# Diagonal blocks copied once each, token norms a projection earlier, and the order of rows and query norms in a DeltaNet layer

## The chip, the cores and the metric

The kernel runs on one core of a Trainium2 chip. The metric is the device time of one execution in microseconds (us). The kernel before takes 2926.78 us, the median of three runs (2923.34 to 2927.39).

The engines are named as the profile names them: PE (TensorE, matmuls; PEld is its weight load), DVE (VectorE), ACT (ScalarE), POOL (GpSimd) and SP (SyncE, which here only issues DMAs). Each engine works through its own queue in order, so an instruction that waits holds up all that stand behind it on that engine. L307 is line 307 of the kernel before; from L183 on, the changed kernel's lines have other numbers.

## The reference

One layer of a trunk on 2048 tokens of width 1024, all in float32: a gated DeltaNet mixer, then a squared-ReLU MLP, then a final norm. Cut to what matters here:

```python
h = rms_norm(x, norm_mix)
proj = h @ w_in                                       # q, k, v, z (8 heads of 128 each), b, a
q, k, v = split(silu(causal_conv4(proj[..., :3 * 1024])))
q, k = l2_normalize(q), l2_normalize(k)
# per head, in chunks:
lower = strict(k_beta @ k.T * decay)
u, w = solve(lower + I, [v * beta, k_beta * exp(gc)]) # unit lower triangular
v_new = u - w @ state
o = q_dec @ state + (q @ k.T * decay) @ v_new
state = state * g_last + k_dec.T @ v_new
x = x + (rms_norm(o) * norm_w * silu(z)) @ w_out
x = x + square(relu(rms_norm(x) @ w_up)) @ w_down
out = rms_norm(x)
```

The kernel uses chunks of 128 tokens, which gives the same numbers as the reference's 64.

## The kernel before

**Blocks, halves, pairs.** The tokens are worked in two blocks of 1024; each goes through `mixer` and then `mlp_block`. A mixer does two halves of 512 tokens (`s`), and in each half four pairs of heads (`h`). A pair has six projections of 512 columns, two heads each of k, q and v (`conv_part`), and each projection is 24 matmuls of 512 columns (L117 to L119, three partial products for each of eight slices). ACT copies the projection out of PSUM (L303, L304), DVE does three multiply-adds of the causal convolution (L307), ACT a tanh (L310) and DVE a product (L311).

**A pair's own work.** From k, `key_matrices` makes the 128x128 matrices `mt` of eight chunks (L429 on PE, L431 and L439 on DVE). `invert_diagonal` inverts the 32x32 diagonal blocks. Four ACT copies (L322) lay the blocks out in `xc`, each block repeated R = 4 times (1024 elements a partition); a DVE transpose (L325) turns them into `pr`; and 31 rows of a product and a sum each (L333, L335) follow on DVE. It is a generator, `rows_of`, that hands the rows out a few at a time. The rest of the inversion (`invert`: L345, L347, L365, L373, L376, L386, L392), transposes of k and v (L469, copied out by ACT at L472) and q times k (L478, L480) belong to `prepare2`. This is a generator too, `stages`, and runs while the next pair projects.

**The chain.** `wind_up` ends a pair while the next one winds up. It does two gate projections (`gate`) and the query norms: ACT squares q (L450), PE sums it (L452), and DVE reads the sum (L454), all through a PSUM bank of the tag `kq`. Then comes `chain`, a recurrence over four chunks of two heads: L496 on PE, `y` on DVE (L498), L505 on PE, `vr` on ACT (L507), L511 on PE, the state on DVE (L512). `fill` puts rows of the next pair between its steps. For the first pair of a block there is no pair to wind up, and its rows all stand at its end in the program.

**Token norms.** During the first half the tokens of the second are normed, 128 in each pair. A DMA fetches `xt` after the first projection; after the second, `norm_transpose` does squares (L180), a reciprocal root, `xn` (L181) and four transposes (L186, PSUM tag `po`), and after the fourth the other four.

**Weights.** In the first half of block 0 each projection's weights come from the input (`wr`, two buffers, L100), POOL splits them into a high and a low part (L90, L91), and SP saves the result (L104); later halves load the saved parts (L109).

**Order.** The program is a list that the framework sorts within each engine's queue by its own estimate, so the written order says only roughly what stands where. PSUM has eight banks: three for projections (`pj`), three for `kq`, two for `po`.

Of the kernel before, what the change touches and what calls it, by code (L numbers as in the profile page):

```python
# [7 lines left out]
F32 = mybir.dt.float32  # L8
# [8 lines left out]
P = 128  # L17
D = 1024
# [4 lines left out]
HB = 512  # L23
HT = HB // P
HP = 2
NC = HP * HT
# [7 lines left out]
def tile_kernel(ctx: ExitStack, tc: tile.TileContext, x, w_in, w_out, w_up, w_down, n_mlp, n_fin, consts, out):  # L34
# [142 lines left out]
    def norm_transpose(i, src, xn, wcol, hh, hl, tag):  # L177

        ssq = sm.tile([P, 1], F32, name="ssq", tag="ssq", bufs=3)
        act.activation(xn, src, AF.Square, accum_out=ssq)  # L180
        dve.tensor_scalar_mul(xn, src, rstd_of(ssq))  # L181
        ti = slice(i * P, (i + 1) * P)
        for k4 in range(0, KS, 4):  # L183
            ps = big(tag)
            for k in range(4):
                pe.transpose(ps[:, k * P:(k + 1) * P], xn[:, (k4 + k) * P:(k4 + k + 1) * P], ident)  # L186
            for k in range(4):
                src_, w = ps[:, k * P:(k + 1) * P], wcol[:, k4 + k:k4 + k + 1]
                act.activation(hh[:, k4 + k, ti], src_, AF.Copy, scale=w)
                dve.scalar_tensor_tensor(hl[:, k4 + k, ti], src_, w, hh[:, k4 + k, ti].bitcast(F32),  # L190
                                         op0=MULT, op1=SUB)
            yield
# [120 lines left out]
    def invert_diagonal(ap, u):  # L313

        R = 32 // NC
        mt = u["mt"]
        xc = wp.tile([P, 32, R, NC], F32, name="xc", tag="xt", bufs=4)
        for b in range(4):  # L320
            r = slice(32 * b, 32 * b + 32)
            act.copy(xc[r], mt[r, :, 32 * b:32 * b + 32].rearrange("p t i -> p i t").unsqueeze(2)  # L322
                     .to_broadcast([32, 32, R, NC]))
        pr = wp.tile([P, 32, 32], F32, name="pr", tag="xt", bufs=4)
        dve.transpose(pr.rearrange("p i j -> p (i j)"), xc.rearrange("p i r t -> p (i r t)"))  # L325
        pool.memset(pr.rearrange("p i j -> p (i j)")[:, 0:1024:33], 1.0)  # L326
        tt = ap.tile([P, NC, 32], F32, name="tt", tag="tt")
        pool.tensor_copy(tt.rearrange("p c j -> p (c j)"), e0)
        yield
        tmp = ap.tile([P, NC, 32], F32, name="tmp", tag="tmp", bufs=1)  # L330
        for i in range(1, 32):
            n = i // R + 1
            dve.tensor_tensor(tmp[:, 0:n, 0:i + 1], tt[:, 0:n, 0:i + 1],  # L333
                              pr[:, i, 0:i + 1].unsqueeze(1).to_broadcast([P, n, i + 1]), op=MULT)
            dve.tensor_reduce(tt[:, 0:n, i], tmp[:, 0:n, 0:i + 1], axis=mybir.AxisListType.X, op=ADD)  # L335
            if i % 2 or i > 16:
                yield
        u["tt"] = tt
# [244 lines left out]
    def mixer(blk, hT):  # L583
        with tc.tile_pool(name="ap", bufs=2) as ap:
# [11 lines left out]
            def wind_up(stages, rows_of, sb, h, hT, qkv, gt, u):  # L596

                def fill(n):
                    for _ in range(n):
                        next(rows_of, None)  # L600

                fill(1)
                z = [gate(ap, hT, h, sb)]
                for _ in stages:
                    pass
                z.append(gate(ap, hT, h + 1, sb))
                for j in range(HP):
                    query_norms(ap, u, qkv[0], j)
                os_ = chain(ap, h, u, fill)
                return [(sb, h + j, os_[j], z[j]) for j in range(HP)]  # L610

            def stages_of(sb, h, hT, qkv, gt, u):
                return prepare2(ap, sb, h, *qkv, gt, u, ub, t64)

            gt = None
            for s in range(2):
                sb = 2 * blk + s
                for h in range(0, NH, HP):
                    qkv, n = [], 0
                    stages = stages_of(*prev) if prev is not None else iter(())  # L620
                    next(stages, None)
                    if s == 0 and h == 0:
                        hT2 = half_tiles()
                    for part in (1, 0, 2):
                        d = ap.tile([P, HP * HB], F32, name=f"c{part}", tag=f"c{part}")
                        qkv.append(d)
                        for j in range(HP):
                            conv_part(ap, hT, part, h + j, d[:, j * HB:(j + 1) * HB], sb)
                            n += 1
                            next(stages, None)  # L630
                            if s == 0 and h == 0 and n <= 3:
                                if n == 1:
                                    gt = {}
                                    g_steps = gates(ap, sb, hT, gt)
                                next(g_steps)


                            if n == 3:
                                u = prepare(ap, sb, h, gt)
                                key_matrices(u, qkv[0], 0)  # L640
                            if n == 4:
                                key_matrices(u, qkv[0], 1)
                                key_norms(u)
                                rows_of = invert_diagonal(ap, u)
                                finish_ready()
                            if blk == 0 and s == 1 and n in (2, 5):
                                split_out(h // HP * 2 + n // 5)
                            if s == 0 and n == 1:
                                xt = wp.tile([P, D], F32, name="xt", tag="xt", bufs=4)
                                r0 = (sb + 1) * HB + h // HP * P  # L650
                                sp.dma_start(xt, x[r0:r0 + P, :])
                            if s == 0 and n == 2:
                                xt_steps = norm_transpose(
                                    h // HP, xt, wp.tile([P, D], F32, name="xn", tag="xt", bufs=4), nmix, *hT2, "po")
                            if s == 0 and n in (2, 4):
                                next(xt_steps)
                            if s == 0 and h == NH - HP and n >= 4:
                                if n == 4:
                                    gt2 = {}
                                    g_steps = gates(ap, sb + 1, hT2, gt2)  # L660
                                next(g_steps, None)
                    if prev is not None:
                        ready += wind_up(stages, rows_of, *prev)
                    for _ in rows_of:
                        pass
                    prev = sb, h, hT, (qkv[1], qkv[0], qkv[2]), gt, u
                if s == 0:
                    for _ in g_steps:
                        pass
                    hT, gt = hT2, gt2  # L670
# [224 lines left out]
```

## Time and profile before

| what | value |
|---|---|
| median of three runs | 2926.78 us |
| the profiled execution's own time | 2925.43 us |
| its span, first to last instruction | 2923.6 us |
| PE busy | 2772.0 us (95%) |
| DVE busy | 1551.5 us (53%) |
| ACT busy | 1024.6 us (35%) |
| POOL busy | 727.9 us (25%) |
| mean granted clock of PE | 0.971 of full speed |

The span is 1.8 us shorter than that execution's time. A share of the whole span says little here: the mixers (0 to about 820 us and about 1500 to 2230 us) and the MLPs have different limits, and PE's idle time lies nearly all in the mixers. So the profile is read stage by stage, by what PE waits for.

### The profile page before, as it was taken

The page shows a single profiled execution, that of the slowest core. Times are in us where ns is not written, and L with a number is a line of the kernel's source. Part 1 is how long each engine was busy: PE and PEld are TensorE (multiplying, and loading weights), DVE is VectorE, ACT ScalarE, POOL GpSimd, SP SyncE. Part 2 cuts the span into 40 slices and gives each one's busy share as a digit, 9 for nine tenths or more (in the row PEclk, how much of TensorE's full clock was granted, in tenths as well). Part 3 has the DMA queues.
Part 4 walks back from the last instruction along what each step waited for, and adds up shares of the span by engine and source line. Part 5 has one row for each costly group of instructions (what it writes and reads, how often), then busy time and mean ns, then how long its engine had stood idle before and what let it go on. Part 6 is the DMA issues. An engine that isn't in the chain of part 4 may idle for free.

```text
span 2923.6 us, 38571 instructions
## 1 busy us (share of the span) xinstructions
PE 2772.0 (95%) x14584; PEld 2294.2 (78%) x14584; DVE 1551.5 (53%) x3814; ACT 1024.6 (35%) x2274; POOL 727.9 (25%) x646
## 2 busy tenths in 40 slices
PE   7688989999999999999998999999999999999998
PEld 6577777777788888888877778788777888888887
DVE  7877677763434334333486776666533333343345
ACT  4455545553221211211246655555422112112112
POOL 6444222110142332332211111111004323323321
PEclk9889999999999999999999999999999999999999
DMA  6444455565521111111254434334572111111111
GB/s 235 174 159 173 159 174 180 180 201 198 185 72 37 58 51 37 58 51 38 64 200 141 145 114 151 139 135 146 173 260 87 44 44 58 45 43 58 46 42 65
DMA packets 77482, 337.52 MB, mean 115 GB/s; under 512 B 8560, under 2 KB 8816, under 8 KB 55792
## 3 DMA queue, kind: packets, MB, share of 16 engines
q1 hardware_dynamic: 58480, 292.98, 29.7%
q10 hardware_dynamic: 18816, 42.08, 4.2%
q8 instruction: 114, 1.87, 0.3%
q14 instruction: 72, 0.59, 0.1%
HBM read 271.98 MB, written 63.05 MB: 115 GB/s over the span
## 4 chain that ended last, share of the span: by engine, by line
PE 72%; DVE 15%; ACT 9%; issue 2%; DMA 1%; POOL 1%; ACTq 0%; POOLq 0%; DVEq 0%; SPq 0%
PE pj L118 12%; PE pj L117 12%; PE pj L119 12%; PE kq L119 8%; PE kq L118 8%; PE kq L117 8%; ACT xc L322 4%; DVE tmp L333 3%; DVE c L307 3%; DVE tt L335 2%; PE kq L511 1%; PE kq L505 1%; PE po L117 1%; PE po L119 1%; PE kq L429 1%
## 5 line engine op out<-in xcount | busy, mean ns | idle before, releaser
L117 PE MATMUL pj<-hh,w 128*128 128x512 f32 x2048 | 822.1, 401 | 0.0
L118 PE MATMUL pj<-hh,w 128*128 128x512 f32 x2048 | 818.9, 400 | 0.0
L119 PE MATMUL pj<-hl,w 128*128 128x512 f32 x2048 | 813.6, 397 | 0.0
L117 PEld LDWEIGHTS pj<-hh,w 128*128 128x128 f32 x2048 | 391.4, 191 | 77.4
L119 PEld LDWEIGHTS pj<-hl,w 128*128 128x128 f32 x2048 | 390.0, 190 | 79.0 <-issue 0.6
L118 PEld LDWEIGHTS pj<-hh,w 128*128 128x128 f32 x2048 | 392.0, 191 | 76.0 <-issue 0.4
L740 ACT ACTIVATE r<-pj 128x512 f32<-128x512 f32 x128 | 76.6, 599 | 1066.6 <-PE pj L119 1066.6
L743 DVE TENSOR_TENSOR ul<-r,uh 128x512 fp32r<-128x512 f32 x128 | 140.9, 1100 | 482.9 <-ACT uh L742 482.9
L119 PE MATMUL kq<-dl,uh 128*128 128x512 f32 x992 | 386.8, 390 | 0.0
L118 PE MATMUL kq<-dh,ul 128*128 128x512 f32 x992 | 386.7, 390 | 0.0
L117 PE MATMUL kq<-dh,uh 128*128 128x512 f32 x992 | 386.6, 390 | 0.0
L783 DVE TENSOR_TENSOR x<-kq,x 128x512 f32<-128x512 f32 x256 | 176.7, 691 | 211.4 <-PE kq L119 208.7
L307 DVE SCALAR_TENSOR_TENSOR c<-raw,cst,c 128x512 f32<-128x512 f32 x288 | 239.4, 835 | 78.3 <-ACT c L304 75.1
L91 POOL TENSOR_TENSOR w<-wr,w 128x1024 fp32r<-128x1024 f32 x106 | 260.8, 2460 | 7.1
L90 POOL TENSOR_SCALAR w<-wr 128x1024 fp32r<-128x1024 f32 x106 | 114.3, 1079 | 590.1 <-PE po L119 299.1
L783 DVE TENSOR_TENSOR x1h<-kq,x1h 128x512 f32<-128x512 f32 x256 | 176.6, 691 | 155.7 <-PE kq L119 155.4
L90 POOL TENSOR_SCALAR dh<-wr 128x1024 fp32r<-128x1024 f32 x62 | 64.2, 1051 | 655.6 <-PE kq L118 622.7
L117 PEld LDWEIGHTS kq<-dh,uh 128*128 128x128 f32 x992 | 186.2, 188 | 40.4 <-DVE rm L145 1.3
L118 PEld LDWEIGHTS kq<-dh,ul 128*128 128x128 f32 x992 | 186.2, 188 | 39.4
L119 PEld LDWEIGHTS kq<-dl,uh 128*128 128x128 f32 x992 | 186.2, 188 | 38.8
L333 DVE TENSOR_TENSOR tmp<-tt,pr 128x2 f32<-128x2 f32 (+30 forms) x496 | 164.5, 332 | 9.9 <-POOL pr L326 0.5
L91 POOL TENSOR_TENSOR dl<-wr,dh 128x1024 fp32r<-128x1024 f32 x62 | 147.3, 2394 | 0.5
(313 smaller groups left out, 3545.4 us busy)
## 6 DMA issues: line engine op xcount, KB each, us to landing
w<-wi SPq DMA_DIRECT2D x96, 1024.0 KB, 4.9
wi<-w SPq DMA_DIRECT2D x32, 1024.0 KB, 4.8
wr<-in_w_up SPq DMA_DIRECT2D x64, 512.0 KB, 3.6
w<-wo SPq DMA_DIRECT2D x32, 1024.0 KB, 5.9
wr<-in_w_down SPq DMA_DIRECT2D x64, 512.0 KB, 3.5
wr<-in_w_in SPq DMA_DIRECT2D x32, 512.0 KB, 5.8
qe<-eg_d ACTq DMA_DIRECT2D x16, 512.0 KB, 3.8
o_d<-z2s ACTq DMA_DIRECT2D x32, 256.0 KB, 2.7
```

Of the source, the lines that this page charges most:

```text
L90: pool.tensor_scalar(dst_h, src, 1.0, 0.0, op0=MULT, op1=ADD)
L91: pool.tensor_tensor(dst_l, src, dst_h.bitcast(F32), op=SUB)
L117: pe.matmul(ps, ah, bh, start=first and i == 0, stop=False)
L118: pe.matmul(ps, al, bh, start=False, stop=False)
L119: pe.matmul(ps, ah, bl, start=False, stop=last and i == n - 1)
L307: dve.scalar_tensor_tensor(dst, raw[:, k:k + HB], cw[:, 4 * f + k:4 * f + k + 1], dst, op0=MULT, op1=ADD)
L322: act.copy(xc[r], mt[r, :, 32 * b:32 * b + 32].rearrange("p t i -> p i t").unsqueeze(2) .to_broadcast([32, 32, R, NC]))
L333: dve.tensor_tensor(tmp[:, 0:n, 0:i + 1], tt[:, 0:n, 0:i + 1], pr[:, i, 0:i + 1].unsqueeze(1).to_broadcast([P, n, i + 1]), op=MULT)
L335: dve.tensor_reduce(tt[:, 0:n, i], tmp[:, 0:n, 0:i + 1], axis=mybir.AxisListType.X, op=ADD)
L740: act.activation(r, ps, AF.Relu)
L743: dve.tensor_tensor(ul[:, hs], r, uh[:, hs].bitcast(F32), op=SUB)
L783: dve.tensor_tensor(dst, ps, dst, op=ADD)
```

## The change

Five things change.

- **Diagonal blocks.** `xc` holds each block once (256 elements a partition), in a buffer of the tag `z`; the DVE transpose reads it four times over through a repeated axis. The `xt` buffers lose one user.
- **Token norms.** `norm_transpose` gives way once more after `xn`. The DMA of `xt` and the buffer for `xn` stand ahead of a pair's projections, squares and `xn` behind the first, the transposes behind the second and the fourth as before.
- **The first pair's rows.** They are no longer run at its end. In the second pair of a block's first half, 12 steps of them stand behind the first projection and the remainder behind the second; `stages` of the first pair starts behind the second projection.
- **Query norms.** They leave `wind_up` and stand behind the pair's own fifth and sixth projection.
- **Half tiles.** `half_tiles()` for the second half is called ahead of the loop.

```diff
@@ norm_transpose
         act.activation(xn, src, AF.Square, accum_out=ssq)
         dve.tensor_scalar_mul(xn, src, rstd_of(ssq))
+        yield
@@ invert_diagonal
-        xc = wp.tile([P, 32, R, NC], F32, name="xc", tag="xt", bufs=4)
+        xc = ap.tile([P, 32, NC], F32, name="xc", tag="z", bufs=1)
...
-            act.copy(xc[r], mt[r, :, 32 * b:32 * b + 32].rearrange("p t i -> p i t").unsqueeze(2)
-                     .to_broadcast([32, 32, R, NC]))
+            act.copy(xc[r], mt[r, :, 32 * b:32 * b + 32].rearrange("p t i -> p i t"))
...
-        dve.transpose(pr.rearrange("p i j -> p (i j)"), xc.rearrange("p i r t -> p (i r t)"))
+        dve.transpose(pr, xc.unsqueeze(2).to_broadcast([P, 32, R, NC]))
@@ wind_up
-                for j in range(HP):
-                    query_norms(ap, u, qkv[0], j)
@@ the loop over pairs
-                    next(stages, None)
+                    late = s == 0 and h == HP
+                    if not late:
+                        next(stages, None)
+                    if s == 0:
+                        xt = wp.tile([P, D], F32, name="xt", tag="xt", bufs=4)
+                        r0 = (sb + 1) * HB + h // HP * P
+                        sp.dma_start(xt, x[r0:r0 + P, :])
+                        xt_steps = norm_transpose(
...
-                            next(stages, None)
+                            if s == 0 and n in (1, 2, 4):
+                                next(xt_steps)
+                            if late and n < 3:
+                                for _ in range(12 * n):
+                                    next(rows_of, None)
+                            if not late or n > 1:
+                                next(stages, None)
...
+                            if n > 4:
+                                query_norms(ap, u, qkv[1], n - 5)
...
-                    for _ in rows_of:
-                        pass
+                    if prev is not None:
+                        for _ in rows_of:
+                            pass
```

What stands in the queues shows it at three places. On PE, in the sixth pair of block 0 (the chain of the states S_88 and S_90), the query sums `kq<-ones,sq` stood in front of the chain's first matmuls. Before:

```order
L118 MATMUL pj<-hh,w_5175 128x512
L119 MATMUL pj<-hl,w_5175 128x512
L452 MATMUL kq<-ones,sq 128x1 x4
L502 MATMUL po<-S_88,qe 128x128
L502 MATMUL po<-S_90,qe 128x128
L117 MATMUL pj<-hh,w_5442 128x512
L118 MATMUL pj<-hh,w_5442 128x512
L119 MATMUL pj<-hl,w_5442 128x512
L117 MATMUL pj<-hh,w_5442 128x512
L452 MATMUL kq<-ones,sq 128x1 x4
L496 MATMUL kq<-S_88,c_3975 128x128
L496 MATMUL kq<-S_90,c_3975 128x128
```

Now they stand two gate projections earlier, and the chain begins:

```order
L118 MATMUL pj<-hh,w_5207 128x512
L119 MATMUL pj<-hl,w_5207 128x512
L496 MATMUL kq<-S_88,c_3991 128x128
L496 MATMUL kq<-S_90,c_3991 128x128
L502 MATMUL po<-S_88,qe 128x128
L502 MATMUL po<-S_90,qe 128x128
L505 MATMUL kq<-y,ub 128x128 x2
L117 MATMUL pj<-hh,w_5458 128x512
```

The matmuls of the next projection that stood between the sums and L505 are behind L505 now; in both orders DVE has about 18 of the next pair's rows in front of `y`.

On DVE, `xn` of the second pair's tokens (block 0) stood among the first pair's rows, beside the second pair's first convolution (c_774). Before:

```order
L139 SCALAR_TENSOR_TENSOR rst<-rt,rst 128x1
L335 TENSOR_REDUCE tt<-tmp 128x4
L135 TENSOR_SCALAR rt<-rst,rh 128x1
L333 TENSOR_TENSOR tmp<-tt,pr 128x4x15
L139 SCALAR_TENSOR_TENSOR rst<-rt,rst 128x1
L335 TENSOR_REDUCE tt<-tmp 128x4
L181 TENSOR_SCALAR xn<-xt,rst 128x1024
L333 TENSOR_TENSOR tmp<-tt,pr 128x4x16
L307 SCALAR_TENSOR_TENSOR c_774<-raw,cst,c_774 128x512
```

Now both first `xn` stand beside the very first convolution (c_264):

```order
L181 TENSOR_SCALAR xn<-xt,rst 128x1024
L139 SCALAR_TENSOR_TENSOR rst<-rt,rst 128x1
L135 TENSOR_SCALAR rt<-rst,rh 128x1
L139 SCALAR_TENSOR_TENSOR rst<-rt,rst 128x1
L135 TENSOR_SCALAR rt<-rst,rh 128x1
L139 SCALAR_TENSOR_TENSOR rst<-rt,rst 128x1
L308 SCALAR_TENSOR_TENSOR c_264<-raw,cst,c_264 128x512
L181 TENSOR_SCALAR xn<-xt,rst 128x1024
L308 SCALAR_TENSOR_TENSOR c_264<-raw,cst,c_264 128x512 x2
L312 SCALAR_TENSOR_TENSOR c_264<-raw,c_264 128x512
```

On SP, in the first half of block 0, loads of raw weights (`wr`) and saves of split ones (`wi`) alternated. Before:

```order
L100 DMA wr<-in_w_in 128x1024
L104 DMA wi_0_120<-w_611 128x2048
L100 DMA wr<-in_w_in 128x1024
L104 DMA wi_1_121<-w_652 128x2048
L100 DMA wr<-in_w_in 128x1024
L104 DMA wi_2_114<-w_779 128x2048
```

Up to about the sixteenth projection they go in twos now:

```order
L100 DMA wr<-in_w_in 128x1024 x2
L104 DMA wi_0_120<-w_611 128x2048
L104 DMA wi_1_121<-w_660 128x2048
L100 DMA wr<-in_w_in 128x1024 x2
L104 DMA wi_2_114<-w_713 128x2048
L104 DMA wi_3_115<-w_821 128x2048
```

A save waits for its split on POOL, so the first load of two is queued behind one split more than it was.

## Rows read from the trace of the kernel before

**Rows 1.** Windows by stage: busy us of PE, PEld, DVE, ACT, POOL; granted clock, DMA, GB/s.

```profile
0.00:158.00 158.00, 115.81 (x616) 94.07 (x616) 120.08 (x273) 72.30 (x136) 81.89 (x92) 0.90 0.59 209
158.00:335.00 177.00, 153.66 (x957) 126.29 (x956) 139.65 (x429) 89.54 (x219) 64.51 (x62) 0.92 0.44 153
335.00:639.00 304.00, 280.12 (x1827) 234.50 (x1826) 215.69 (x620) 163.75 (x387) 64.89 (x84) 0.96 0.54 186
639.00:1505.00 866.00, 857.40 (x3968) 707.95 (x3968) 348.10 (x638) 199.94 (x427) 227.33 (x138) 0.99 0.26 84
1505.00:1613.00 108.00, 94.52 (x548) 77.55 (x547) 76.46 (x246) 61.72 (x119) 15.04 (x37) 0.95 0.49 172
1613.00:2061.00 448.00, 424.98 (x2781) 355.19 (x2779) 315.71 (x1048) 253.29 (x606) 49.00 (x99) 0.97 0.40 140
```

**Rows 2.** PE's waits in the whole span: us in total, times, longest us.

```profile
PE po L186 <- DVE xn L181: 25.9, 2, 15.9
PE kq L496 <- DVE n L454: 19.8, 8, 5.5
PE po L469 <- ACT vt L472: 13.0, 10, 5.0
PE kq L452 <- ACT sq L450: 11.7, 6, 3.2
PE po L186 <- ACT o L530: 11.5, 3, 8.1
PE kq L172 <- DVE xn L167: 8.5, 1, 8.5
...
PE kq L505 <- DVE y L498: 5.5, 10, 0.9
```

**Rows 3.** PE's timeline: start us, us; idle before and its releaser in brackets.

```profile
96.94 0.47 PE L186 MATMUL po<-cst,xn 128*128 128x128 f32 x1 [15.94 <-DVE xn L181]
...
564.49 0.58 PE L496 MATMUL kq<-S,c 128*128 128x128 f32 x1 [3.93 <-DVE n L454]
```

**Rows 4.** ACT's copies by line and shape: count, busy us, mean ns, idle before.

```profile
L322 ACT COPY xc<-mt 32x1024 f32<-32x1024 f32 x64 | 129.9, 2029 | 31.6 <-DVE mt L439 24.0 <-DMA o_d<-z2s 6.7
...
L347 ACT COPY tcm<-tr 128x256 f32<-128x256 f32 x16 | 10.8, 675 | 9.8 <-DVE tr L345 4.7 <-DVE rq L139 3.1 <-DVE nq L524 1.9
```

**Rows 5.** DVE's block transposes by line and shape, columns as in rows 4.

```profile
L325 DVE STREAM_TRANSPOSE pr<-xc 128x1024 f32<-128x1024 f32 x16 | 19.9, 1246 | 38.1 <-ACT xc L322 38.1
...
L345 DVE STREAM_TRANSPOSE tr<-tt 128x256 f32<-128x256 f32 x16 | 7.1, 441 | 0.3
```

**Rows 6.** Windows of DVE alone, up to each block's first chain: busy us, then clock.

```profile
29.00:158.00 129.00, 99.07 (x240) 0.87 0.57 199
...
1506.00:1613.00 107.00, 75.57 (x243) 0.95 0.48 170
```

**Rows 7.** DVE's timeline in the sixth pair of block 0, from pr to y.

```profile
551.33 1.25 DVE L325 STREAM_TRANSPOSE pr<-xc 128x1024 f32<-128x1024 f32 x1 [2.07 <-ACT xc L322]
...
558.61 2.21 DVE L333 TENSOR_TENSOR tmp<-tt,pr 128x33 f32<-128x33 f32 x1
...
564.28 0.15 DVE L454 TENSOR_SCALAR n<-kq 128x4 f32<-128x4 f32 x1
...
565.91 0.60 DVE L498 SCALAR_TENSOR_TENSOR y<-kq,neg,vt 128x128 f32<-128x128 f32 x2
```

**Rows 8.** DVE's convolution step in 0 to 639 us, then in 1505 to 2061 us.

```profile
L307 DVE SCALAR_TENSOR_TENSOR c<-raw,cst,c 128x512 f32<-128x512 f32 x144 | 132.3, 922 | 35.7 <-ACT c L304 34.2
...
L307 DVE SCALAR_TENSOR_TENSOR c<-raw,cst,c 128x512 f32<-128x512 f32 x144 | 107.1, 747 | 42.6 <-ACT c L304 40.9
```

**Rows 9.** POOL's split in 0 to 639 us; raw weight loads: count, KB, us to landing.

```profile
L91 POOL TENSOR_TENSOR w<-wr,w 128x1024 fp32r<-128x1024 f32 x40 | 97.9, 2448 | 1.6
L90 POOL TENSOR_SCALAR w<-wr 128x1024 fp32r<-128x1024 f32 x40 | 44.9, 1122 | 75.5 <-PE pj L119 69.7 <-DMA dt__498<-gc_d 2.5 <-DMA wr<-in_w_in 2.0
...
wr<-in_w_in SPq DMA_DIRECT2D x32, 512.0 KB, 5.8
```

More of the change, by code (lines that the diff above doesn't have):

```diff
@@ L613, in stages_of @@
                 return prepare2(ap, sb, h, *qkv, gt, u, ub, t64)
-            gt = None
+            gt, hT2 = None, half_tiles()
             for s in range(2):
@@ L620, in mixer @@
                     stages = stages_of(*prev) if prev is not None else iter(())
-                    next(stages, None)
-                    if s == 0 and h == 0:
-                        hT2 = half_tiles()
+                    late = s == 0 and h == HP
[6 more added lines that the diff above has]
+                        xt_steps = norm_transpose(
+                            h // HP, xt, wp.tile([P, D], F32, name="xn", tag="xt", bufs=4), nmix, *hT2, "po")
                     for part in (1, 0, 2):
@@ L647, in mixer @@
                                 split_out(h // HP * 2 + n // 5)
[L648 to L656, printed above, removed]
+                            if n > 4:
+                                query_norms(ap, u, qkv[1], n - 5)
                             if s == 0 and h == NH - HP and n >= 4:
```

## The prediction

> **What bounds the kernel now.** I read the windows by stage first. From 639 to 1505 us (end of the first mixer, MLP) PE is busy 857.4 of 866 us at a clock of 0.99; nothing in the change touches that stage or its twin after 2061 us. The mixers are different [rows 1]: PE is idle 42.2 us in 0 to 158 us, 23.3 in 158 to 335, 23.9 in 335 to 639, 13.5 in 1505 to 1613 and 23.0 in 1613 to 2061, together 126 us, and there the granted clock is 0.90 to 0.97, a mean of stretches at 2.4 GHz and at 1.2. Weighing the missing clock with PE's busy time, (1 - 0.90) x 115.8 and so on, gives 11.6, 12.3, 11.2, 4.7 and 12.7 us: 52 us more. So about 178 us is all that could be won, and each idle us comes with some 0.4 us of slow clock behind it.
>
> Second, what PE waits for [rows 2]. Four of these waits are named by the change: the second half's transposes for `xn` (25.9 us in two waits) and for `po` banks that the chain's outputs hold (11.5, mostly one of 8.1); the chain's L496 for a `kq` bank that DVE's L454 has not read (19.8 in eight); the query sums for ACT's squares (11.7); transposes L469 for `po` banks that ACT empties (13.0). They add to 82 us. The 8.5 at the start (L172) stays.
>
> Third, whether the engine waited for is itself full. Up to the first chain of block 0 DVE is busy 99.1 of 129 us; in block 1 it is 75.6 of 107 [rows 6]. So in the first two pairs of each block a removed wait of PE can gain only what DVE has free, about 30 us each, and part of that is latency between engines. This is why I do not take the 82 us.
>
> **The change part by part.** All sums are against the profiled execution, 2925.43 us (span 2923.6 plus 1.8 around it); the median is 1.35 us above it.
>
> *Copies.* A copy of 1024 elements takes 2.03 us, about 2 ns each [rows 4]. The copy of 256 is not in the trace. Nearest is L347, 256 elements read in another order than they lie in, 0.675 us [rows 4]; the bounds are a quarter of the old one, 0.51, and the old one unchanged, 2.03. I take 0.675: four a pair fall from 8.1 to 2.7 us, on ACT 5.4 us a pair, 87 us over 16 pairs. Most of it lies beside other work: the transpose L325 waits 38.1 us for these copies in 16 pairs, 2.4 a pair [rows 5], and that, with some of the 13.0 us of L469, is what can show. On the reason for 2 ns: the Trainium skill (Advanced Engine Details and Errata, SBUF Cachelines) says that at least two accesses must fall into a 16-byte line for full speed, and the source here steps by a whole chunk of 128 elements. That step stays, so by the page the 256 cost as much apiece as the 1024; L347's price holds that already. The sum does not change.
>
> *Repeated read.* L325 takes 1.25 us for 1024 elements and L345 0.44 us for 256 [rows 5], so about 1.05 ns each plus a fixed part. It still puts out 1024, so I cost the repeated axis at nothing; the bounds are nothing and, if a repeated read halved its pace as a stepped one does ACT's, 1.2 us a pair, 20 us of DVE in all, half of it on the path.
>
> *First two pairs of block 0 (to 158 us).* The second pair's `xn` is computed beside the first, so the wait of 15.9 us [rows 3] goes; so do a query sum's wait (about 2.9, a quarter of 11.7) and part of L469's. Late next is DVE. New in front of the first chain are a second reciprocal root and `xn` by the first convolution (about 3 us; up to 7 if two of the short steps meet a split of 2.45 us [rows 9]) and some nine rows of the second pair that stood behind `y` (rows run at 0.7 us each with all that is between them [rows 7], bare ones less: 4 us). Of DVE's 30 free us these take 7, and I leave 10 for latencies that stay: gates, key matrices, and the steps of the first pair's inversion, which now stand close together on PE behind the second pair's projections, with little to run in their waits. Gain 13 us. Bounds: 5 (DVE keeps 18 us of idle time) and 20 (it keeps 3).
>
> *First two pairs of block 1 (1505 to 1613).* The same without splits on POOL. PE's idle time and slow clock are 18.2 us [rows 1]; DVE has 31 us free, less 5 for what is added. About 6 us go back in the close inversion. Gain 12; bounds 6 and 16.
>
> *158 to 335 us.* The wait of 8.1 us for `po` banks stays in kind: the transposes stand 1.54 instead of 1.71 projections behind the chain's end, while DVE has some 3 us less in front of the chain's norms. I count 1.5 us, another 1.5 from the longest L496 wait (5.5), 2 from clock. Gain 5; bounds -2 and 14.
>
> *The other pairs, 335 to 639 and 1613 to 2061.* L496 no longer waits for L454, but the step behind it, L505, waits for `y`, and `y` stands behind about 18 rows before and after. In the sixth pair PE waits 3.9 us at L496 [rows 3] because L454 comes out at 564.28, 13 us after `pr` [rows 7]. With shorter copies `pr` comes 2.4 us earlier [rows 5]; the six matmuls that stood ahead of L505 no longer fill the wait, 6 x 0.22 = 1.3 us (0.22 from 857.4/3968 [rows 1]). So about 1.1 us a pair remains of 3.9, and the cover lost here is why. Three pairs in block 0 give 3.5, L469 and other small waits 2, the last pair's query sum, which has no chain's rows ahead of it, 2.4, clock 1: 9 us, bounds 3 and 16. In block 1 the waits are smaller: 2, plus 2.6 for the last query sum, plus 1.5 of clock: 6 us, bounds 0 and 13.
>
> *SP's queue.* Loads in twos put the first of two behind one split more, 1.12 + 2.45 = 3.6 us [rows 9]. Two splits and one landing (5.8 us [rows 9]) are 12.9 us; up to the first chain 14 projections share 158 us, over 20 us for two. So I cost it at nothing; the cover is gone only where bare projections run close, at 24 x 0.22 x 2 = 10.6 us for two, some four times: up to 9 us.
>
> Sum: 13 + 12 + 5 + 9 + 6 = 45 us. 2925.4 - 45 is 2880.4, on the median's scale 2881.8; I say 2881.
>
> **The rivals.**
>
> A. *The waits go and nothing takes their place.* If DVE keeps pace, the 82 us go with 0.4 x 82 = 33 of clock; less what the chain's `y` keeps (some 30), that is 85: 2842. For it: DVE is at half load after the first pairs. Against: rows 6 and the 18 rows ahead of `y`. Chance 0.14.
>
> B. *DVE is the bound of the first pairs.* The first pair's rows now lie wholly among projections that each bring a split. L307 takes 922 ns where POOL splits and 747 where it does not [rows 8]; the row at 558.61 took 2.21 us beside neighbours of 0.2 [rows 7]. Over 144 steps that is 25 us, and rows suffer alike. If all 14 splits stop DVE for their whole 2.45 us instead of about half, that is 17 us in block 0: the 13 become -4; block 1 gives 6, the others keep 12. Total gain 14: 2913. The Trainium skill (SBUF — State Buffer, SBUF: two separate sides) states an exclusive lock between GpSimd and a DVE instruction with two SBUF inputs, held for a whole instruction; the row of 2.21 us agrees, and by that rule a fuller DVE queue meets more splits. Chance 0.17.
>
> C. *Slower: weights starve PE.* POOL holds a split behind the memset of `pr` or the product with `qe`, both of which wait for others; with loads in twos a late split delays two loads and PE waits for weights. Price: each of eight twos late by 3.6 + 5.8 = 9.4 us is 75 us against the 45: 2957. It decides above 5.6 us a two. Against: no matmul of a projection waits for weights in rows 2, and POOL is busy 82 of 158 us. Chance 0.05.
>
> D. *The copies do not get shorter, or the repeated read costs what they save.* Then ACT's or DVE's share in all pairs goes, some 10 us: 2892. Same side. Chance 0.06.
>
> **How the numbers follow.** Forecast 0.58 (gains of 30 to 62 us: 2865 to 2897), A 0.14, B 0.17, C 0.05, D 0.06. The bounds of the parts add to 12 and 79. From 2850 to 2908 the range holds the forecast, D, half of A and half of B, about 0.8. A measurement of this kernel tells 0.2%, 5.9 us, from no change. Faster by more than that: the forecast, A, D and all of B but its end: 0.91; within: 0.04; slower: 0.05.
>
> **What would show it.** Right: waits of L186 for `xn` and of L452 gone; L496's wait small and L505's for `y` grown to 2 or 3 us a pair in block 0; the first chain at about 145 us instead of 158, DVE busier than 0.8 up to it, and PE waiting at L365 for `tcm`; the copy at 0.5 to 0.7 us, the transpose still at 1.25. Wrong: PE waiting at L117 (C), DVE full to the first chain (B), no wait at L505 (A).

## The result and the profile after

The changed kernel takes 2905.49 us (median of four runs, 2903.75 to 2912.12) against 2925.06 for the kernel before in the same comparison: a ratio of 0.9939, 95% interval 0.9919 to 0.9959. It gains some 20 us, less than half of the 45 that were forecast. The direction and the range held, but the first of the experiments below shows that single terms missed by more than the sum did, in both directions.

The windows by stage of the changed kernel, with bounds at the same places of the program as [rows 1] (busy us of PE, PEld, DVE, ACT, POOL; granted clock, DMA, GB/s):

```profile
0.00:158.00 158.00, 126.17 (x621) 102.38 (x622) 116.31 (x290) 62.48 (x138) 79.60 (x90) 0.87 0.55 203
158.00:343.00 185.00, 155.70 (x960) 129.08 (x959) 149.64 (x420) 78.04 (x217) 66.16 (x62) 0.90 0.44 151
343.00:643.00 300.00, 279.93 (x1827) 236.66 (x1827) 218.32 (x610) 140.86 (x387) 65.71 (x85) 0.96 0.54 186
643.00:1505.00 862.00, 851.40 (x3959) 702.80 (x3958) 352.26 (x638) 198.46 (x425) 226.02 (x138) 0.99 0.26 85
1505.00:1606.00 101.00, 95.73 (x554) 78.94 (x553) 80.44 (x281) 52.00 (x122) 14.89 (x37) 0.97 0.48 175
1606.00:2043.00 437.00, 421.28 (x2787) 353.69 (x2786) 317.65 (x1016) 218.78 (x604) 47.88 (x99) 0.98 0.42 144
```

From one chain's start to the next, the stretches that the sum was made of have changed like this (the changed kernel's bounds 158.3, 343.3, 642.9, 683.1, 1606.0, 2042.6; before 157.6, 335.1, 639.1, 680.4, 1612.7, 2061.3): the first pairs of block 0 are 0.7 us longer, the next two chains 7.5 longer, the other pairs of block 0 4.3 shorter, block 0's end to the first chain of block 1 9.3 shorter, block 1's other pairs 12.0 shorter, the ends 2.3 shorter: 19.7 us, the difference of the spans (2923.6 and 2903.9). Of the 9.3 us, 2.1 lie ahead of block 1's first pairs; from ACT's first copy of block 1 out of PSUM (1504.4 us before, 1504.9 now) to the chain it is 7.2. So block 1 gave 19 where 18 were forecast, and block 0, 3.9 us longer up to its seventh chain, gave none of its 27.

What PE waits for in the changed kernel (total us, times, longest):

```profile
PE kq L505 <- DVE y L498: 27.3, 12, 8.6
PE kq L365 <- ACT tcm L347: 26.4, 11, 5.5
...
PE po L187 <- ACT o L530: 7.7, 1, 7.7
PE po L269 <- DVE cc L434: 6.0, 1, 6.0
PE po L237 <- ACT kt L472: 5.5, 2, 4.7
PE pj L118 <- POOL w L91: 5.4, 3, 2.1
...
PE pj L117 <- POOL w L90: 4.7, 2, 3.3
```

Against [rows 2] the waits that the change names are gone: 25.9 us for `xn`, 19.8 at L496, nearly all of the 11.7 for the squares. In their place stand 27.3 us at L505 for `y` (5.5 before), 26.4 at L365 for `tcm`, and 10.1 us of projections that wait for weights, which before had no such wait. PE's idle time fell in all from 151.6 to 132.8 us, while its slow clock rose from 60.8 to 65.5 us. (Here and below, slow clock is the time lost at 1.2 GHz, half of each us in which PE is busy at that clock.)

The operations themselves came out as costed. Copies and transposes of the changed kernel, by line and shape (count, busy us, mean ns, idle before):

```profile
L323 ACT COPY xc<-mt 32x256 f32<-32x256 f32 x64 | 40.9, 639 | 28.9 <-DVE mt L439 24.8 <-DMA o_d<-z2s 3.3
```

```profile
L325 DVE STREAM_TRANSPOSE pr<-xc 128x1024 f32<-128x1024 f32 x16 | 19.9, 1244 | 37.7 <-ACT xc L323 37.7
```

A copy takes 639 ns where it took 2029, and the repeated read costs nothing (1244 ns, 1246 before [rows 5]). But DVE still stands 37.7 us empty for the copies (38.1 before), though they are 89 us shorter in all. The idle time in front of the transpose was no measure of what the copies cost.

### The profile page after: what moved, and what is told of

The parts are those of the page before. It is cut to its first block, busy times and chain, and to the rows that moved or that the text cites. A ratio compares the mean times of both kernels' runs of the same rounds, so it can differ in the third digit from the quotient of the medians.

```text
span 2903.9 us, 38562 instructions
## 1 busy us (share of the span) xinstructions
PE 2771.1 (95%) x14584; PEld 2298.0 (79%) x14584; DVE 1572.2 (54%) x3814; ACT 933.6 (32%) x2274; POOL 724.4 (25%) x646
## 4 chain that ended last, share of the span: by engine, by line
PE 74%; DVE 16%; ACT 4%; DMA 2%; issue 2%; POOL 1%; ACTq 0%; SPq 0%; POOLq 0%; DVEq 0%
PE pj L119 12%; PE pj L118 12%; PE pj L117 12%; PE kq L119 8%; PE kq L118 8%; PE kq L117 8%; DVE tmp L333 4%; DVE c L308 3%; DVE tt L335 2%; PE kq L511 1%; PE po L117 1%; PE po L119 1%; PE po L118 1%; PE kq L505 1%; PE kq L429 1%
## 5 line engine op out<-in xcount | busy, mean ns | idle before, releaser
L117 PEld LDWEIGHTS kq<-dh,uh 128*128 128x128 f32 x992 | 186.3, 188 | 40.3 <-DVE rm L145 1.4
L333 DVE TENSOR_TENSOR tmp<-tt,pr 128x2 f32<-128x2 f32 (+30 forms) x496 | 183.8, 370 | 12.2 <-POOL pr L326 1.6
```

Source lines behind the costliest of these rows:

```text
L117: pe.matmul(ps, ah, bh, start=first and i == 0, stop=False)
```

## The experiments

### One edit after the other

First the copies alone, on the kernel before:

```diff
+        xc = ap.tile([P, 32, NC], F32, name="xc", tag="z", bufs=1)
...
+            act.copy(xc[r], mt[r, :, 32 * b:32 * b + 32].rearrange("p t i -> p i t"))
...
+        dve.transpose(pr, xc.unsqueeze(2).to_broadcast([P, 32, R, NC]))
```

> The kernel before with the diagonal blocks copied once, and nothing else. Theory P (the terms of the prediction): four copies a pair shorter by 1.35 us each bring about 10 us, most of it at the chain's start, so about 2915 us against 2925. Theory Q (the changed kernel's trace, where the chain's first wait only moved from L496 to L505 and kept its size): the transpose comes earlier, but DVE fills the time with convolution steps and splits still stop its rows; gain 2 to 5 us, about 2921.

Measured: 2881.72 us, ratio 0.9859 (0.9834 to 0.9884). The copies alone give 42 us, twice what all five edits give. Then the token norms as well:

```diff
...
+                            if s == 0 and n in (1, 2, 4):
+                                next(xt_steps)
...
```

> Copies, and the token norms behind the first projection (with the half tiles taken ahead); rows and query norms as before. P: the two waits for xn (15.9 and 10.0 us) go and DVE takes some of it back, a further 12 to 17 us, about 2901. Q: in block 0 the norm of the second pair meets no full DVE as long as the first pair's rows stand where they stood, so the gain is the same or larger than with all five edits: 2898 to 2904.

Measured: 2874.06 us, ratio 0.9831 (0.9808 to 0.9853); some 8 us more. The two kernels that lack one edit each, first without the spread rows:

```diff
-                            if late and n < 3:
-                                for _ in range(12 * n):
-                                    next(rows_of, None)
...
```

> The changed kernel with one edit undone: the first pair's rows stand at its end again. P: spreading the rows is part of the gain of the first pairs, so without it about 5 us slower than all five, 2910. Q: the rows behind the second pair's first projections make DVE full from 81 to 129 us, POOL's tail copies wait for DVE, the splits wait behind them (10.4 us at the projections' matmuls) and the inversion runs close together at half clock (12 us); without that edit block 0 gains 8 to 15 us: about 2893 to 2898, and no wait of a projection for weights.

Measured: 2889.98 us, ratio 0.9887 (0.9866 to 0.9908). And without the moved query norms:

```diff
-                            if n > 4:
-                                query_norms(ap, u, qkv[1], n - 5)
...
+                for j in range(HP):
+                    query_norms(ap, u, qkv[0], j)
```

> The changed kernel with the query norms back at the end of the pair, ahead of the chain. P: their place is worth the last pairs' waits for the squares (2.4 and 2.6 us) and some of L496's, about 6 us: 2911. Q: the same for the last pairs, 4 to 5 us, and nothing at the chain's start, where y decides: 2909 to 2910. If the two agree, it only prices the edit.

Measured: 2889.58 us, ratio 0.9882 (0.9863 to 0.99). So from copies and token norms at 2874, the spread rows cost 15.5 us, the moved query norms 15.9, and both together 31. Q had the sign of the rows right and their size nearly (8 to 15 us). Both theories were wrong about the query norms and about the copies, and P's further 12 to 17 us for the token norms were too many.

### Why the copies give so much

> The kernel with only the copies changed (2881.7 us), but xc left in a buffer of the tag xt, where it stood before. Theory A (ACT's time): four shorter copies take 5.5 us a pair off the way from mt to pr, and the pair's length follows; the buffer plays no part: 2879 to 2885. Theory B (the buffer): part of the 42 us comes from xt having one user less, so this is at least 8 us slower, 2890 or more.

```diff
+        xc = wp.tile([P, 32, NC], F32, name="xc", tag="xt", bufs=4)
...
```

Measured: 2879.36 us, ratio 0.9842 (0.9826 to 0.9857), the same as with the other buffer. The buffer plays no part.

> The kernel with only the copies changed, each of the four copies made twice, the same data: 5.1 us of ACT a pair instead of 2.6 (8.1 before). Theory A: the way from mt to pr is on the loop that sets a pair's length, so 2.6 us a pair come back at the rate at which 5.5 us gave 42: about 20 us, 2896 to 2906. Theory B (the buffer, or only the sorted order): 2881 to 2886.

```diff
+            act.copy(xc[r], mt[r, :, 32 * b:32 * b + 32].rearrange("p t i -> p i t"))
             act.copy(xc[r], mt[r, :, 32 * b:32 * b + 32].rearrange("p t i -> p i t"))
```

Measured: 2898.18 us, ratio 0.9904 (0.9885 to 0.9922). 2.6 us of ACT a pair cost 16 to 19 us (against the two kernels with single copies), about what A said. The traces show why. ACT's timeline in a pair of block 1, first of the kernel before (start us, us; idle before in brackets):

```profile
1887.66 2.01 ACT L322 COPY xc<-mt 32x1024 f32<-32x1024 f32 x1 [3.35 <-DVE mt L439]
...
1895.47 1.99 ACT L322 COPY xc<-mt 32x1024 f32<-32x1024 f32 x1
1897.48 0.59 ACT L303 COPY raw<-pj 128x512 f32<-128x512 f32 x1
1898.10 0.69 ACT L304 ACTIVATE c<-pj,cst 128x512 f32<-128x512 f32 x1
1898.81 4.14 ACT L322 COPY xc<-mt 32x1024 f32<-32x1024 f32 x2
```

Then the same pair with the copies alone changed:

```profile
1852.57 0.64 ACT L322 COPY xc<-mt 32x256 f32<-32x256 f32 x1 [3.34 <-DVE mt L438]
...
1859.02 1.95 ACT L322 COPY xc<-mt 32x256 f32<-32x256 f32 x3
```

From the first copy's start to the last one's end it is 15.3 us before and 8.4 after. `pr`, which ended 7.5 us ahead of the chain's first L496, ends 13.6 us ahead. All of the 5.5 us of shorter copies, and two evictions (copies out of PSUM) that no longer come between them, lie on the way from `mt` over `xc`, `pr` and the rows to `tcm`. Where that way sets a pair's length the pair gets shorter: the middle pairs of block 0 fall from 75 to 71.5 us, those of block 1 from 73 to 68. Not all of it counts everywhere: over 16 pairs the ways from `mt` to the last copy are 96 us shorter, the kernel 42. In the profiled executions that gain is 26.5 us of PE's idle time and 16.8 of slow clock. DVE's idle time in front of the transpose, 38.1 us before, is still 35.2 with the copies alone changed:

```profile
L324 DVE STREAM_TRANSPOSE pr<-xc 128x1024 f32<-128x1024 f32 x16 | 19.9, 1244 | 35.2 <-ACT xc L322 35.2
```

### Why the moved query norms cost

Two causes were left: the square that now stands on ACT ahead of three copies, and the sums that no longer stand in front of the chain. Three kernels speak to it. The norms behind the next pair's first two projections, in neither place:

```diff
...
+                            if prev is not None and n < 3:
+                                query_norms(ap, prev[5], prev[3][0], n - 1)
...
```

> Copies and token norms (2874), with a pair's query norms behind the first and second projection of the next pair: neither between mt and the copies on ACT (where the change put them) nor in front of the chain (where they stood). Theory A: the changed place cost 16 us because a square and its sums stand ahead of three copies and of the transposes; here that falls away and the seventh pairs' waits for the squares (5.0 and 6.3 us, with slow clock) go: 2858 to 2868. Theory G (the sums in front of the chain are cover for y; without them the chain waits for y wherever they go): 2880 to 2892.

Measured: 2911.64 us, ratio 0.9963 (0.9947 to 0.9979): some 38 us slower than with the norms in the old place (copies and token norms, 2874). That speaks for G and against A, but G's bounds (2880 to 2892) are missed by 20 us. The chains of the seventh pairs wait 6.0 and 6.9 us at L505 here, 2.0 and 1.5 with early norms and unspread rows; the rest of the excess stays open. The copies on DVE as well, so that ACT's queue can't hold them:

> Both: copies on DVE and query norms behind the next pair's first two projections. Theory A: the gains add, 2842 to 2856. Theories F and G: no better than the better of the two alone, 2870 or more.

Measured: 2898.97 us, ratio 0.9919 (0.9902 to 0.9935). PE waits 40.3 us at L505 there, with copies that in most pairs end 1.6 us behind `mt`; with the norms in the old place and the same copies the kernel takes 2870.54 us (the first version below). Last, the early norm and the old one both, the same work twice:

```diff
                 z.append(gate(ap, hT, h + 1, sb))
+                for j in range(HP):
+                    query_norms(ap, u, qkv[0], j)
```

> Copies, token norms and query norms behind the pair's own projections (2890), with the whole query norm made a second time in its old place in front of the chain, the same values: about 0.65 us of squares on ACT and 16 sums of 3 us on PE more in each pair, some 50 us of work in all. Theory G (the sums in front of the chain are cover: the chain's first y is queued behind some 20 rows on DVE and cannot come earlier, so work put in front of the chain costs nothing there and what is taken away is waited for): the wait at L505 goes back to under 1 us a pair and the time stays within 8 us of 2890 although 50 us of work are added. Theory A (the early square ahead of the copies on ACT is the cost): the second norm is extra work on a path that is late already, 2910 to 2940.

Measured: 2883.47 us, ratio 0.986 (0.9831 to 0.989). With some 50 us of work added it is 6.5 us faster than without. In the profiled executions PE's own work is 34 us longer, its idle time 25 us shorter and its slow clock 12 us. PE's waits without the second norm (the kernel that lacks the spread rows):

```profile
PE kq L505 <- DVE y L498: 25.0, 10, 7.1
PE kq L365 <- ACT tcm L347: 16.0, 9, 4.5
```

And with it:

```profile
PE kq L496 <- DVE n L454: 9.8, 4, 6.0
...
PE kq L365 <- ACT tcm L347: 5.3, 7, 2.0
...
PE kq L505 <- DVE y L498: 3.6, 4, 1.7
```

So the sums of a pair, 3.1 us (8 in the program, 16 matmuls in the trace), are cover: work that fills a wait. `y` is queued on DVE behind 18 to 21 rows, and the rows can't begin before `pr`, so in the middle pairs of the kernels with short copies on ACT the first `y` starts 12.7 to 16.8 us behind `pr`. Sums in front of the chain cost nothing there. Put elsewhere, they leave a wait at L505, of their own length in block 0's middle pairs (3.4 us) and of 0.8 us in block 1's, and at L365 the pair waits once more (16.0 us in all, 5.3 with both norms). The seventh pairs are the exception: there the old place waits for the squares, and with early norms they take 75.3 and 71.1 us in place of 82.3 and 75.3. Another part can be the square: in the kernel with early norms and unspread rows ACT does it ahead of three copies, behind an eviction that waited for PE.

```profile
1866.03 0.63 ACT L472 ACTIVATE kt<-po,egl 128x128 f32<-128x128 f32 x2 [0.53 <-PE po L469]
...
1868.57 0.68 ACT L450 ACTIVATE sq<-c 128x512 f32<-128x512 f32 x1
1869.27 1.95 ACT L323 COPY xc<-mt 32x256 f32<-32x256 f32 x3
```

In block 1's last four pairs `mt` to the last copy is 9.4 us there and 8.4 with copies and token norms alone (9.2 and 8.4 in three pairs of block 0), so about 1 us of such a pair's way is the square's. No run takes the square alone away, so its share of the 15.9 us is not measured.

### Why the spread rows cost

In block 0 the changed kernel waits for weights and then for `tcm`. POOL's timeline in the second pair:

```profile
97.02 0.19 POOL L302 COPY raw<-tail 128x3 f32<-128x3 f32 x1 [5.54 <-DVE tt L335]
97.18 1.13 POOL L90 TENSOR_SCALAR w<-wr 128x1024 fp32r<-128x1024 f32 x1
98.26 0.19 POOL L306 COPY tail<-raw 128x3 f32<-128x3 f32 x1
98.41 2.34 POOL L91 TENSOR_TENSOR w<-wr,w 128x1024 fp32r<-128x1024 f32 x1
```

PE's at the same time:

```profile
98.36 0.80 PE L117 MATMUL pj<-hh,w 128*128 128x512 f32 x1 [3.31 <-POOL w L90]
100.81 0.80 PE L118 MATMUL pj<-hh,w 128*128 128x512 f32 x1 [1.65 <-POOL w L91]
```

The split stands behind a tiny copy (L302) that waits 5.54 us for a buffer which DVE, full of rows, has not read. Taking that copy and its twin off POOL:

```diff
-        pool.tensor_copy(raw[:, 0:3], tail[:, f, :])
+        act.copy(raw[:, 0:3], tail[:, f, :])
...
-        pool.tensor_copy(tail[:, f, :], raw[:, HB:HB + 3])
+        act.copy(tail[:, f, :], raw[:, HB:HB + 3])
```

> The kernel with all five edits (2905), the two small copies of the convolution's tail on ACT instead of POOL, so that no split stands behind a copy that waits for DVE. Theory S (the splits' place in POOL's queue makes the weights late): the 10.4 us that projections wait for w go and some of the slow clock after them: 2890 to 2898. Theory D (DVE is full from 81 to 129 us): the wait moves to L365 for tcm, the first chain starts within 3 us of 158: 2902 to 2910.

Measured: 2907.08 us, ratio 0.9936 (0.9919 to 0.9953), no gain, as D said. Its bound on the first chain did not hold (149.0 us, 9 earlier), but that is clock: up to there this profile has 12.1 us less of slow clock than the changed kernel's, and 2.5 us more of idle time. Later the gain is lost again, and PE waits 17 us more at L505 (44.3 in all); that the copies on ACT cause this is likely but was not tested. PE's waits of that kernel up to 149 us:

```profile
PE kq L365 <- ACT tcm L347: 13.2, 1, 13.2
...
PE pj L118 <- POOL w L91: 3.6, 2, 2.4
```

Most of the weights come in time, and PE waits for `tcm` instead (13.2 us where it was 5.5): up to L365, DVE is the bound. What fills it is tested by taking the two-input subtraction away from the six splits of that pair:

```diff
+        if cheap:
+            pool.tensor_scalar(wh, raw, 1.0, 0.0, op0=MULT, op1=ADD)
+            pool.tensor_scalar(wl, raw, 0.0, 0.0, op0=MULT, op1=ADD)
```

> All five edits, but in the second pair of block 0 (heads 2 and 3 of q, k and v) the low part of the weights is not computed: POOL writes zeros with a one-input operation of about 1.05 us where the subtraction took 2.4. Theory D: the rows of 1.0 to 2.6 us beside a subtraction fall to 0.2 to 0.4, some 10 us of DVE, so the first chain starts at 145 to 150 us and the whole is 2890 to 2897. Theory S: the splits are as late as before behind the tail copies, only 1.4 us shorter: 2900 to 2906.

Measured: 2897.55 us, ratio 0.9905 (0.9872 to 0.9937), its runs from 2888 to 2907. The first chain starts at 140.6 us instead of 158.3. Of these 17.7 us 8.9 lie ahead of L365, which comes at 119.8 us instead of 128.7 because the rows end sooner. The other 8.8 lie behind it, where this profile has 10.0 us less of slow clock, which the cheap splits don't explain. The rows over 2 us fall from six to two, and the two stand beside full splits, those of the gates' weights; one beside a one-input operation takes as long as that does, 1.0 to 1.1 us. DVE's timeline:

```profile
97.13 0.25 DVE L337 TENSOR_TENSOR tmp<-tt,pr 128x100 f32<-128x100 f32 x1
...
104.94 1.10 DVE L337 TENSOR_TENSOR tmp<-tt,pr 128x189 f32<-128x189 f32 x1
106.59 2.07 DVE L337 TENSOR_TENSOR tmp<-tt,pr 128x196 f32<-128x196 f32 x1
110.03 2.57 DVE L337 TENSOR_TENSOR tmp<-tt,pr 128x232 f32<-128x232 f32 x1
```

POOL's:

```profile
104.79 1.04 POOL L90 TENSOR_SCALAR w<-wr 128x1024 fp32r<-128x1024 f32 x1
...
106.11 2.35 POOL L91 TENSOR_TENSOR w<-wr,w 128x1024 fp32r<-128x1024 f32 x1
...
109.66 2.68 POOL L91 TENSOR_TENSOR w<-wr,w 128x1024 fp32r<-128x1024 f32 x1
```

In all kernels with full splits the rows of the first pair take 43 to 50 us from the first product to the last sum, and L365 comes at 123 to 132 us wherever they stand. The spread rows therefore bring L365 no sooner (128.7 us; 128.1 without that edit), while the steps behind it, which begin a projection later, take longer from L365 to the first L496: 29.6 us against 23.1 in block 0, 24.8 against 19.9 in block 1.

In block 0 the difference is clock: 11.7 of the 29.6 us, and 1.7 of the 23.1, are slow clock. In block 1 slow clock and idle time make 1.7 us each of the 4.9. Windows of the changed kernel behind L365 (columns as in the first table of this section):

```profile
129.00:152.00 23.00, 23.00 (x171) 20.16 (x170) 6.86 (x39) 10.33 (x27) 8.49 (x6) 0.50 0.43 161
152.00:158.00 6.00, 6.00 (x35) 5.24 (x34) 4.62 (x17) 4.51 (x12) 0.16 (x1) 0.99 0.00 0
```

PE is busy without a gap for 23 us and has 1.2 GHz all through, which costs 11.5 us. The clock fell at 128.3 us, at the end of the 5.5 us that PE waited for `tcm`. The order of work alone doesn't decide this: the last two kernels below have the same order on PE, DVE, ACT and POOL up to here, and in the second alone the clock is low. The copies on DVE, from 134 us:

```profile
134.00:142.00 8.00, 7.25 (x95) 6.35 (x89) 4.17 (x19) 4.43 (x10) 0.19 (x1) 1.00 0.51 166
142.00:150.00 8.00, 8.00 (x42) 6.79 (x41) 7.13 (x23) 0.60 (x1) 5.10 (x3) 1.00 0.01 2
```

The same with the moved square:

```profile
134.00:142.00 8.00, 7.72 (x88) 6.41 (x85) 2.70 (x5) 4.27 (x10) 0.71 (x2) 0.57 0.59 199
142.00:150.00 8.00, 8.00 (x48) 7.47 (x47) 4.44 (x26) 0.58 (x1) 0.00 (x0) 0.58 0.00 0
```

Such a stretch (14 to 24 us at 1.2 GHz, begun between 126 and 136 us) stands in four of the fifteen profiles: in the changed kernel and the one with the query norms put back, which have spread rows, but also in the one with the norms behind the next pair's projections and in the last version below, which have none. Over whole executions the spread rows do go with slow clock. Two pairs of kernels differ in this edit alone, and each pair's profiles are 16.4 us apart: idle time makes 3.1 and 0.4 us of that, slow clock 14.7 and 17.0. It is not one execution's luck: the mean granted clock is 0.973 to 0.975 in the changed kernel's runs and 0.976 to 0.979 without the spread rows, and in the other pair of kernels 0.973 to 0.977 and 0.978 to 0.980. So the edit's cost is mostly clock; why the clock is lower with it stays open.

### A faster version

> Copies and token norms (2874), with the four copies of a pair on DVE right behind mt instead of on ACT, where three of them stand behind transposes' and projections' evictions. Theory A (the way from mt to tcm sets a pair's length; 38.9 us in block 1, 42.4 in block 0): pr comes about 6 us earlier at 1.5 us more DVE a pair; in block 0 pairs fall from 71.5 towards the 67 us that block 1's pairs need, block 1's gain 1 us each: 2855 to 2866. Theory F (after the shorter copies the way no longer sets it, PE's own work does): 2870 to 2878.

```diff
-            act.copy(xc[r], mt[r, :, 32 * b:32 * b + 32].rearrange("p t i -> p i t"))
+            dve.tensor_copy(xc[r], mt[r, :, 32 * b:32 * b + 32].rearrange("p t i -> p i t"))
```

Measured: 2870.54 us, ratio 0.9816 (0.9795 to 0.9837). `pr` ends 20.7 us ahead of the chain where it was 13.6, but F is nearer: block 1's middle pairs take 67.5 us, two of them with 0.03 us of idle time, so PE's own work bounds them, and shortening the way further brings little. From copies and token norms on ACT (2874) the difference is within the noise.

```diff
+                            if s == 1 and h == NH - HP and n == 2:
+                                sq2 = prev[5]["sq"] = wp.tile([P, D], F32, name="sq2", tag="xt", bufs=4)
+                                act.activation(sq2, prev[3][0], AF.Square)
...
```

> Copies on DVE and token norms (2870.5), with one square moved: in the seventh pair of each block, where the sums wait 2.5 and 6.0 us for squares that stand on ACT behind casts waiting for a DMA, q is squared once in a buffer of its own while the last pair projects; the sums keep their place in front of the chain. If that wait is idle time with slow clock behind it and nothing else is late there: 2858 to 2866. If y is late anyway (theory G for this pair): 2868 to 2872.

Measured: 2870.39 us, ratio 0.9819 (0.9793 to 0.9845), no difference that can be told. The two stretches before the seventh chains do shrink (72.5 to 67.8 us and 75.0 to 66.0), but its profile has 8.1 us more of slow clock in the first pairs, the stretch just shown, and 5.3 us more between 629 and 1592 us. Both kernels beat the changed one by 35 us, and the one before, in their own comparisons, by 51 and 55.

## Why the prediction was right and wrong

- **Copies.** The price was right (0.675 taken, 0.639 measured; nothing for the repeated read). The step that failed is the one that turned it into time: I took what DVE stood idle in front of L325, 2.4 us a pair, as all that could show, because "most of it lies beside other work", and of these 38 us the parts held only some 10. The copies alone give 42. They lie between `mt` and `pr` one after the other, and where that way sets a pair's length most of their 5.5 us counts: some 3.5 us a pair in the middle of block 0, 5 in block 1. That 38 is near to 42 is luck: the idle time is still 35.2 us with the short copies (38.1 before [rows 5]). It measures a waiting engine, not the length of the way.
- **First two pairs of block 0: 13 us forecast, none measured.** Idle time fell by 10.4 us, near the forecast. The step that failed is the clock: I let slow clock fall with idle time, some 0.4 us for each, and priced no rise, but it rose by 10.4 us (7.8 to 18.2). The condition was right ("late next is DVE"): DVE kept nothing free where it mattered, and L365 came only 1.9 us sooner (128.7, 130.6 before). Over 29 to 158 us DVE is busy 96 us, yet from 81 to 129 without a pause; a mean over a window hid it. Rival B named this and its mechanism, which is there (the first pair's products take 22.0 us, 16.7 before). Its -4 is the nearest to -0.7, but in part by luck, for B says nothing of the clock. Rival C's mechanism, weights late behind POOL's queue, was there with 10.1 us, and when most of it was taken away `tcm` was late instead.
- **First two pairs of block 1: 12 forecast, 7.2 measured** in the stretch that was named, inside its bounds. Without the spread rows it is 12.8.
- **158 to 335 us: 5 forecast, a loss of 7.5.** The wait for `po` banks stayed in kind as I said (7.7 us). In place of the 5.5 us at L496 stand 8.6 at L505, and with them 4.6 at L365 (2.3 before) and 4.7 at L237. The step that failed is the 1.5 us taken from L496's wait as a gain: the wait moved to L505 and grew.
- **The other pairs: 9 and 6 forecast, 4.3 and 12.0 measured.** I saw that the sums were cover for L505 and priced what stays by the six matmuls, 1.3 us; the cover is 3.1 us and its loss comes back a second time at L365. With the query norms in their old place, and all else as changed, block 1's term is 20.2 us. Block 0's is 3.4, no larger, for there the seventh pair gives back what the middle ones gain (81.3 us, 75.2 with the norms moved).
- **SP's queue in twos** cost little: of the 10.1 us at the projections' matmuls, the first wait (1.6 us) stands behind a split that waited 1.5 us for its load. The others stand behind splits that waited for DVE.
- **The signs.** The waits for `xn` and for the squares went, L505's grew and L365 waits for `tcm`, as said. The first chain comes at 158.3 us and not at 145, and DVE's share up to it is 0.75 and not over 0.8.
- **The sum.** Block 0's first two terms missed by 26 us, as much as the sum did. By edits, the copies were under by some 30 us, and two edits taken as gains of a few us cost 16 each. That 45 is near the 50 of copies and token norms together is chance.

On the rule that the prediction cited from the Trainium skill (SBUF — State Buffer, SBUF: two separate sides), the exclusive lock: the runs agree with it as far as they go, since the rows' stops of over 2 us went with the two-input subtraction and stayed where that stayed; the one-input operations stop rows too, for their own shorter time (1.10 us beside 1.04). The other rule cited from the Trainium skill (Advanced Engine Details and Errata, SBUF Cachelines), that full speed wants two accesses in a line, is consistent with 2.5 ns an element at 256 and 2.0 at 1024, but no run here has this copy from a source without the step.

## What to carry to other kernels

- Price a shorter step by following the way from its input to the next thing that PE needs, in the trace's times, pair by pair, and not by the idle time of the engine behind it: here that idle time hardly changed while the kernel got 42 us shorter. Where PE's own work already sets the length, the shorter way gains nothing.
- An instruction that reads ready data in front of a chain may be cover. Before moving it, look at what the chain's first result is queued behind; if that is fixed by something else, the move only uncovers a wait. Doing the work twice is a quick test of it.
- Undo the edits of a bundle one at a time: here one edit gave more than the bundle, and two cost 31 us. Split what is left into idle time and slow clock: one of the two costs was nearly all clock, and a sum of waits would not have shown it.

## What the runs showed of the hardware

Two profiled executions with the same order of work on PE, DVE, ACT and POOL up to that point differ in granted clock: at 134 to 150 us one has 1.00 and the other 0.57 to 0.58, with PE busy 15.3 and 15.7 of the 16 us. In the changed kernel PE is busy without a gap for 23 us and the clock stays at 1.2 GHz. A copy on ACT of a quarter of the elements takes 0.31 of the time (639 of 2029 ns), not 0.25. On DVE the same copy takes 538 ns in the mean and 382 in the median, with single ones up to 2.5 us.
